# Eight row buffers for an expert gather, one half of an output projection taken block by block, and tile steps moved between two stages of a decoder layer

## The chip, the cores and the metric

The kernel runs on one core of one Trainium2 chip. The metric is the device time of one execution in microseconds (us), the median of several runs. The engines are PE (matmul), PEld (its weight load), DVE (vector), ACT (scalar), POOL (gpsimd) and SP (sync, which here only issues DMAs).

## The reference

One layer of a decoder, 512 tokens of width 1024, all in float32: a token mixing step (mLSTM heads beside sliding-window attention), a cross-attention into 256 memory tokens, and a PEER layer that retrieves experts. The change touches the end of the second and the third:

```python
h = h + memory_cross_attention(rmsnorm(h, g_cross[l]), rmsnorm(mem, g_mem[l]), ...)   # ends in o @ w_o
h = h + peer_ffn(rmsnorm(h, g_ffn[l]), w_pq[l], sub_keys1[l], sub_keys2[l], expert_down[l], expert_up[l])
return rmsnorm(h, g_final)

# inside peer_ffn, for each token: 8 heads, 16 experts of 128 x 128 per head
    eidx = jnp.take_along_axis(cand_i, pos, axis=-1)
    g = jax.nn.softmax(top_s, axis=-1)
    u = expert_down[eidx]
    a = jax.nn.gelu(jnp.einsum('thkd,td->thk', u, xb), approximate=False)
    coef = (g * a)
    return jnp.einsum('thk,thkd->td', coef, expert_up[eidx])
```

## The kernel before

The 512 tokens are four blocks of 128 (NB = 4). Products are made with three matmuls each (high part by high, high by low, low by high of operands split in two), so that float32 accuracy is kept. A split is a copy on ACT (the high part) and a subtraction on DVE (the low part).

`front` does the mixing, `cross` the cross-attention in the order of the string `CROSS`. Its last four items, x0 to x3, are `project`: two halves n of the output columns, two halves hf of the contraction; for each it loads a weight of 1 MB (`load_w`) and multiplies it with all four blocks; when hf is 1, `resid` adds the result to the residual `c.h`. Then `norm_T` normalizes each block (a square with a sum on ACT, `rsqrt` on DVE and POOL, a scaling on DVE), transposes it on PE and splits it into `xhi` and `xlo`.

The experts are done in two ways. Block 0 **gathers**: `gather` is a generator of 256 steps. Each step fetches one row per token (128 rows of 4 KB, 512 KB) with an indirect DMA issued by POOL (`fetch`, L685) into one of the buffers of tag `rows`, and one DVE operation consumes it: 128 dot products with `down` (L691), then 128 accumulations with `up` into `gacc` (L699, L701). Blocks 1 to 3 are **dense**: all 128 tiles of 128 experts are multiplied with all 384 tokens. A `Down` tile takes 8 k-steps of three matmuls (L757 to L759) and ends in a gelu; an `up_tile` multiplies the gelu by the gates and `up_mm` (L823 to L825) accumulates it. `down_t` and `up` come in loads of 1 MB for two tiles (`draw`, `uraw`).

The gates of the dense blocks are a matrix of 16384 experts by tokens. Block 1's is made by 128 scattering indirect DMAs on POOL (`scatter`, L614), those of blocks 2 and 3 by one-hot matmuls (`gating`, 32 steps for each block, L666; the one-hot operands come from ACT, L649 and L650, and DVE, L645 and L665).

The stages follow each other: `peer_topk` (queries, scores, top 16 of each head, on PE, ACT and above all DVE), `gating`, then the loop over `up_order()`. `Early.fill(k)` puts k k-steps of the first SP = 68 `Down` tiles between the steps of the first two: FRT[i] in each of the 16 `stage1` calls, FEND behind them, FGT with each gating step. Those tiles are spilled to DRAM and read again. The other 60 are made in the loop, five ahead (LEAD). In the loop, `step(ga, ...)` calls for gather steps, 256 spread over the first 122 of 128 tiles. Behind the loop stand the rest of the gather, the loads of the residual (`hb`) and four calls of `finish` (add, square, `rsqrt`, scaling, store), block 0 with `gacc` and then blocks 1 to 3, whose last two tiles' matmuls are held back and done block by block.

The order in the program is not the order on the engines: the framework plans each engine's queue beforehand (`schedule_with_timeline_sim=True`), by program order among what its plan takes to be ready, and inserts the waits. At run time each queue is in order. The rows buffers are memory slots: a fetch waits for the DVE operation that used the slot last. Tiles of a pool that opens where another closed wait for the last readers of that other one. On SP all loads and stores of the hardware queue stand in one line.

Of the kernel before, what the change touches and what calls it, by code (L numbers as in the profile page):

```python
# [21 lines left out]
P = 128  # L22
# [18 lines left out]
UG = 4  # L41
FRT = [16] + [24] * 15
FEND = 5 * KT
FGT = 2
SP = (sum(FRT) + FEND + (ND - NS) * 32 * FGT) // KT
SG = SP // UG
assert SP == SG * UG and (sum(FRT) + FEND) % KT == 0

GST = 122

# [6 lines left out]

CROSS = "m0 o0 K1 K0 V0 V1 n0 q0 s0 s1 q1 s2 p0 s3 p1 p2 p3 x0 x1 x2 x3"
HP = 400
# [345 lines left out]
def cross(c):  # L405
    nc, a, ps, xp = c.nc, c.a, c.ps, c.xp
    V, A, T = nc.vector, nc.scalar, nc.tensor
    qh, ql, probs, acc, wo = {}, {}, {}, {}, {}

# [50 lines left out]

    def project(i):
        n, hf = divmod(i, 2)
        if hf == 0:
            acc[n] = [ps.tile([P, 512], F32, tag="b", name=f"acc_t{b}") for b in range(NB)]
        w = load_w(c, a["w_xo"][n, hf], 512)
        for b in range(NB):
            mm3_tm(c, acc[n][b], w, slice(0, 512), hf, b)
            if hf:
                resid(c, b, n, acc[n][b])

    ops = {"n": norm, "K": lambda n: mem_k(c, n), "V": lambda n: mem_v(c, n), "m": lambda _: mem_norm(c),
           "o": lambda _: mix_out(c), "q": query, "s": scores, "p": values, "x": project}
    for op in CROSS.split():
        ops[op[0]](int(op[1]))


# [145 lines left out]

def gating(c, early):

    nc, ps, gs, mp = c.nc, c.ps, c.gs, c.mp
    V, A, T = nc.vector, nc.scalar, nc.tensor
    for b in range(NG + NS, NB):
# [24 lines left out]

        oh = [onehot(q) for q in range(3)]
        for q in range(32):
            if q % 8 == 0:
# [16 lines left out]
            with c.tc.issue_after(mm.ins):  # L672
                early.fill(FGT)


def gather(c):
# [6 lines left out]
    def fetch(src, j):  # L683
        r = gp.tile([P, D], F32, tag="rows", bufs=5, name="rows")
        G.indirect_dma_start(out=r, out_offset=None, in_=src,  # L685
                             in_offset=bass.IndirectOffsetOnAxis(ap=c.eidx[:, j:j + 1], axis=0))
        return r
# [328 lines left out]
def body(tc, a, out, dbg=None):  # L1016
# [3 lines left out]
    with ExitStack() as st:  # L1020
# [23 lines left out]
        with ExitStack() as hs:  # L1044
# [14 lines left out]
            c.xn0 = c.mp.tile([P, D], F32, name="xn0")  # L1059
            norm_T(c, [c.h[:, b] for b in range(NB)], D, c.xhi, c.xlo, xn0=c.xn0)  # L1060
            for b in range(NB):
                nc.sync.dma_start(c.hd[b], c.h[:, b])
        c.m2 = st.enter_context(pool("routes"))
        c.dp = st.enter_context(pool("down"))
        gel = []
# [10 lines left out]
        c.gl = st.enter_context(pool("gels"))  # L1076
        with pool("gather", side="right") as c.gp:
            with pool("gating") as c.gs:
                gating(c, early)
            ga = gather(c)  # L1080
            c.up = st.enter_context(pool("up"))
# [3 lines left out]
            acc = [[pst_[2 * b], pst_[2 * b + 1]] for b in range(ND)]  # L1085
            last = []
            for u, i2 in enumerate(up_order()):
                ahead(made_by(u) - len(gel))
                with tc.issue_after(c.dl.ins):
                    step(ga, 2 * P * (u + 1) // GST - 2 * P * u // GST)  # L1090
                parts = up_tile(c, u, i2, gel, acc)
                if u >= NK - 2:
                    last.append(parts)
                else:
                    for b in range(ND):
                        up_mm(c, u, parts, acc, b)
            step(ga, 2 * P)
            c.hb = []
            for b in range(NB):
                c.hb.append(c.gp.tile([P, D], F32, tag="rows", bufs=5, name="hb"))  # L1100
                nc.sync.dma_start(c.hb[b], c.hd[b])
# [29 lines left out]
def step(it, n):  # L1131
    for _ in range(n):
        next(it, None)
# [49 lines left out]
```

## Time and profile before

| | us |
|---|---|
| median of 3 runs (lowest to highest) | 1703.74 (1701.27 to 1706.47) |
| the profiled execution | 1698.9 |
| its span, first to last instruction | 1697.1 |
| PE busy in it | 1629.7 |
| DVE busy in it | 1236.8 |

The profiled execution lies 4.8 us below the median of the runs; what lies around its span is 1.8 us. "Busy" counts the time in which at least one instruction of an engine runs. PEclk is the TensorE clock that was granted, as a share of full speed. A wait is put down to what ended it. L numbers are lines of the kernel.

### The profile page before, as it was taken

What the parts mean: (1) busy time and instruction counts of PE and PEld (TensorE: products, weight loads), DVE (VectorE), ACT (ScalarE), POOL (GpSimd) and SP (SyncE); (2) the same over time, 40 slices, a digit from 0 to 9 for tenths busy, and PEclk for the clock granted to TensorE, in tenths of its full rate; (3) what the DMA queues carried; (4) which work ended last, traced back from release to release, by engine and by line L of the source; (5) the groups of instructions that cost most, each with busy time, mean ns of one, the idle gap of its engine ahead of it and who ended that gap; (6) DMA issues with size and microseconds to landing.
All of it is one profiled execution on the core that took longest, in us unless ns stands there. A gap on an engine that the chain in (4) does not pass through costs nothing.

```text
span 1697.1 us, 23023 instructions
## 1 busy us (share of the span) xinstructions
PE 1629.7 (96%) x8366; PEld 1424.7 (84%) x8368; DVE 1236.8 (73%) x2701; ACT 720.6 (42%) x1206; POOL 582.6 (34%) x427
## 2 busy tenths in 40 slices
PE   7999999999999999989999999999999999999990
PEld 5776588877999999989998888888888888888880
DVE  5536565464687876878858888877878788888897
ACT  5434544343445443478853333333333333333331
POOL 2000000000008686758003443334444344334563
PEclk9999999999999999999999999999999999999995
DMA  5136044224245554559769888989989999998887
GB/s 209 74 139 233 26 149 174 75 103 149 73 158 143 137 137 94 137 187 267 211 217 407 329 325 338 329 337 355 354 321 340 354 331 344 348 339 321 308 308 263
DMA packets 149105, 400.58 MB, mean 236 GB/s; under 512 B 28144, under 2 KB 62080, under 8 KB 136320
## 3 DMA queue, kind: packets, MB, share of 16 engines
q1 hardware_dynamic: 89232, 255.76, 41.6%
q0 software_dynamic: 55360, 134.32, 23.9%
q10 hardware_dynamic: 4400, 9.04, 1.5%
q8 instruction: 65, 1.06, 0.2%
q14 instruction: 48, 0.39, 0.1%
HBM read 356.28 MB, written 42.80 MB: 235 GB/s over the span
## 4 chain that ended last, share of the span: by engine, by line
PE 89%; issue 3%; POOL 2%; DVE 2%; DMA 2%; ACT 1%; DVEq 0%; POOLq 0%; ACTq 0%
PE acc_d L757 10%; PE acc_d L759 10%; PE acc_d L758 10%; PE acc_u L824 9%; PE acc_u L825 9%; PE acc_u L823 9%; PE acc_f L923 4%; PE acc_f L925 4%; PE acc_f L924 4%; PE w L666 3%; PE acc_t L936 2%; PE acc_t L938 2%; PE acc_t L937 2%; POOL rows L685 2%; DMA rows<-in_up_dram,eidx 1%
## 5 line engine op out<-in xcount | busy, mean ns | idle before, releaser
L757 PE MATMUL acc_d<-xhi,dh 128*128 128x384 f32 x1024 | 351.0, 343 | 2.8 <-ACT dh L708 1.8
L759 PE MATMUL acc_d<-xhi,dl 128*128 128x384 f32 x1024 | 345.1, 338 | 0.6 <-DVE dl L746 0.6
L758 PE MATMUL acc_d<-xlo,dh 128*128 128x384 f32 x1024 | 344.3, 336 | 0.0
L824 PE MATMUL acc_u<-ul,ch 128*128 128x512 f32 x762 | 297.8, 391 | 0.0
L825 PE MATMUL acc_u<-uh,cl 128*128 128x512 f32 x762 | 297.2, 391 | 0.0
L685 POOL DMA_INDIRECT rows<-in_down_r_dram,eidx x128 | 168.1, 1313 | 344.0 <-DVE dots L691 316.0
L614 POOL DMA_INDIRECT wd<-gg,ei x128 | 214.5, 1676 | 158.6 <-DVE ei L608 114.4
L823 PE MATMUL acc_u<-uh,ch 128*128 128x512 f32 x762 | 257.2, 390 | 0.0
L746 DVE TENSOR_TENSOR dl<-draw,dh 128x1024 fp32r<-128x1024 f32 x128 | 156.4, 1222 | 123.0 <-ACT dh L708 112.3
L685 POOL DMA_INDIRECT rows<-in_up_dram,eidx x128 | 175.7, 1373 | 199.6 <-DVE gacc L701 181.4
L708 ACT CAST dh<-draw 128x1024 fp32r<-128x1024 f32 x128 | 134.2, 1050 | 239.3 <-PE acc_d L758 201.3
L811 ACT CAST ch<-cf 128x384 fp32r<-128x384 f32 x127 | 65.2, 514 | 368.8 <-issue 334.2
L757 PEld LDWEIGHTS acc_d<-xhi,dh 128*128 128x128 f32 x1024 | 193.3, 189 | 7.1 <-ACT dh L708 2.2
L758 PEld LDWEIGHTS acc_d<-xlo,dh 128*128 128x128 f32 x1024 | 193.4, 189 | 3.7
L759 PEld LDWEIGHTS acc_d<-xhi,dl 128*128 128x128 f32 x1024 | 193.0, 189 | 2.6 <-DVE dl L746 1.2
L701 DVE SCALAR_TENSOR_TENSOR gacc<-rows,coef,gacc 128x1024 f32<-128x1024 f32 x127 | 162.6, 1280 | 7.5 <-DMA rows<-in_up_dram,eidx 6.5
L825 PEld LDWEIGHTS acc_u<-uh,cl 128*128 128x128 f32 x762 | 143.0, 188 | 29.4
L824 PEld LDWEIGHTS acc_u<-ul,ch 128*128 128x128 f32 x762 | 143.0, 188 | 28.9
L823 PEld LDWEIGHTS acc_u<-uh,ch 128*128 128x128 f32 x762 | 142.7, 188 | 27.1
L802 DVE TENSOR_TENSOR ul<-uraw,uh 128x1024 fp32r<-128x1024 f32 x127 | 154.9, 1220 | 7.8 <-ACT uh L708 6.7
L691 DVE CUSTOM_DVE_ANT_0 rows<-rows,xn 128x1024 f32<-128x1024 f32 x128 | 153.8, 1219 | 0.0
L812 DVE TENSOR_TENSOR cl<-cf,ch 128x384 fp32r<-128x384 f32 x127 | 70.7, 558 | 90.9 <-ACT ch L811 76.3
(333 smaller groups left out, 2659.9 us busy)
## 6 DMA issues: line engine op xcount, KB each, us to landing
draw<-in_down_t_dram SPq DMA_DIRECT2D x64, 1024.0 KB
uraw<-in_up_dram SPq DMA_DIRECT2D x64, 1024.0 KB
wt<-wd SPq DMA_DIRECT2D x96, 256.0 KB
wd<-stg SPq DMA_DIRECT2D x8, 2048.0 KB
gd<-gsp SPq DMA_DIRECT2D x17, 768.0 KB
gsr<-gd SPq DMA_DIRECT2D x17, 768.0 KB
wd<-zero ACTq DMA_DIRECT2D x1, 8192.0 KB
raw<-in_w_pq_dram SPq DMA_DIRECT2D x8, 1024.0 KB
```

Of the source, the lines that this page charges most:

```text
L614: i = G.indirect_dma_start(out=out, out_offset=bass.IndirectOffsetOnAxis(ap=ei[:, h, k:k + 1], axis=0), in_=c.gg[:, NG, hh, k:k + 1], in_o ...
L685: G.indirect_dma_start(out=r, out_offset=None, in_=src, in_offset=bass.IndirectOffsetOnAxis(ap=c.eidx[:, j:j + 1], axis=0))
L691: V.tensor_tensor_reduce(r, r, c.xn0, 1.0, 0.0, op0=ALU.mult, op1=ALU.add, accum_out=dots[:, j:j + 1])
L701: V.scalar_tensor_tensor(c.gacc, r, coef[:, j:j + 1], c.gacc, op0=ALU.mult, op1=ALU.add)
L746: c.dl = nc.vector.tensor_tensor(self.lo, raw, f32(self.hi), op=ALU.subtract)
L757: T.matmul(acc[:, :TD], self.hi[:, ks], c.xhi[:, k, NG * P:], start=(k == 0), stop=False)
L758: T.matmul(acc[:, :TD], self.hi[:, ks], c.xlo[:, k, NG * P:], start=False, stop=False)
L759: T.matmul(acc[:, :TD], self.lo[:, ks], c.xhi[:, k, NG * P:], start=False, stop=(k == KT - 1))
L802: V.tensor_tensor(lo, raw, f32(hi), op=ALU.subtract)
L823: T.matmul(acc[b][n], ch[:, t], hi[:, d], start=st, stop=False)
L824: T.matmul(acc[b][n], ch[:, t], lo[:, d], start=False, stop=False)
L825: T.matmul(acc[b][n], cl[:, t], hi[:, d], start=False, stop=sp)
```

## The change

- `rows` gets 8 buffers in place of 5, and the generator is made before `gating`, which gets it as an argument: in its last block (b = 3) every fourth step calls one gather step, 8 in all. The loop then spreads 248 steps over its first 122 tiles.
- x0 to x3 leave `CROSS`, and `project` becomes a function that runs after the pools of `cross` have closed. Its first half (n = 0) is as before. The weights of the second half get buffers of their own (`w2`), and each block does both halves of the contraction, `resid` and then, as the argument of `norm_T`, its normalization, before the next block begins. The pools `routes` and `down` open ahead of it.
- FRT falls from 24 to 20 k-steps in 14 of 16 places and FEND from 40 to 24; FGT rises from 2 to 3, and FGT0 = 8 k-steps are put between the first three one-hot tiles and the first gating step. SP stays 68: 544 k-steps either way.

```diff
-FRT = [16] + [24] * 15
-FEND = 5 * KT
-FGT = 2
-SP = (sum(FRT) + FEND + (ND - NS) * 32 * FGT) // KT
+FRT = [16] + [20] * 14 + [24]
+FEND = 3 * KT
+FGT0 = KT
+FGT = 3
+SP = (sum(FRT) + FEND + FGT0 + (ND - NS) * 32 * FGT) // KT
+GEV = 4
-CROSS = "m0 o0 K1 K0 V0 V1 n0 q0 s0 s1 q1 s2 p0 s3 p1 p2 p3 x0 x1 x2 x3"
+CROSS = "m0 o0 K1 K0 V0 V1 n0 q0 s0 s1 q1 s2 p0 s3 p1 p2 p3"
-    def project(i):
-        n, hf = divmod(i, 2)
-        if hf == 0:
-            acc[n] = [ps.tile([P, 512], F32, tag="b", name=f"acc_t{b}") for b in range(NB)]
-        w = load_w(c, a["w_xo"][n, hf], 512)
-        for b in range(NB):
-            mm3_tm(c, acc[n][b], w, slice(0, 512), hf, b)
-            if hf:
-                resid(c, b, n, acc[n][b])
+def project(c):
+    ps, a = c.ps, c.a
+    acc = [ps.tile([P, 512], F32, tag="b", name=f"acc_t{b}") for b in range(NB)]
+    w2 = []
+    for hf in range(2):
+        w = load_w(c, a["w_xo"][0, hf], 512)
+        for b in range(NB):
+            mm3_tm(c, acc[b], w, slice(0, 512), hf, b)
+            if hf:
+                resid(c, b, 0, acc[b])
+        w2.append(load_w(c, a["w_xo"][1, hf], 512, pool=c.w2))
+    def block(b):
+        acc = ps.tile([P, 512], F32, tag="b", name=f"acc_t{b}")
+        for hf in range(2):
+            mm3_tm(c, acc, w2[hf], slice(0, 512), hf, b)
+        resid(c, b, 1, acc)
+        return c.h[:, b]
+    norm_T(c, [lambda b=b: block(b) for b in range(NB)], D, c.xhi, c.xlo, xn0=c.xn0)
...
 def gating(c, early, ga):
+        if b == NG + NS:
+            early.fill(FGT0)
         for q in range(32):
...
             with c.tc.issue_after(mm.ins):
                 early.fill(FGT)
+                if b == NB - 1 and q % GEV == GEV - 1:
+                    step(ga, 1)
...
-        r = gp.tile([P, D], F32, tag="rows", bufs=5, name="rows")
+        r = gp.tile([P, D], F32, tag="rows", bufs=8, name="rows")
...
-            norm_T(c, [c.h[:, b] for b in range(NB)], D, c.xhi, c.xlo, xn0=c.xn0)
+            c.m2 = st.enter_context(pool("routes"))
+            c.dp = st.enter_context(pool("down"))
+            with pool("project") as c.w2:
+                project(c)
...
+            ga = gather(c)
             with pool("gating") as c.gs:
-                gating(c, early)
-            ga = gather(c)
+                gating(c, early, ga)
...
+            g0 = 32 // GEV
-                    step(ga, 2 * P * (u + 1) // GST - 2 * P * u // GST)
+                    step(ga, (2 * P - g0) * (u + 1) // GST - (2 * P - g0) * u // GST)
...
-                c.hb.append(c.gp.tile([P, D], F32, tag="rows", bufs=5, name="hb"))
+                c.hb.append(c.gp.tile([P, D], F32, tag="rows", bufs=8, name="hb"))
```

## Rows read from the trace of the kernel before

**Rows 1.** The page: busy time by engine, and the shares of the chain that ended last.
```profile
PE 1629.7 (96%) x8366; PEld 1424.7 (84%) x8368; DVE 1236.8 (73%) x2701; ACT 720.6 (42%) x1206; POOL 582.6 (34%) x427
...
PE 89%; issue 3%; POOL 2%; DVE 2%; DMA 2%; ACT 1%; DVEq 0%; POOLq 0%; ACTq 0%
```

**Rows 2.** Busy time by stretch, cut at the seams of the stages: mixing and cross-attention to the end of the projection's matmuls, the seam to the top-k, the top-k, the seam to the gating, the gating, the seam to the loop, the loop, what lies behind PE's last matmul. The columns are the stretch, its length, the busy time of PE, PEld, DVE, ACT and POOL, each with its instructions, the granted clock, the DMA share and GB/s.
```profile
0.00:407.00 407.00, 393.26 (x1880) 300.82 (x1883) 216.22 (x453) 178.08 (x349) 20.78 (x38) 1.00 0.37 132
407.00:420.00 13.00, 8.93 (x50) 8.09 (x49) 8.71 (x10) 5.90 (x9) 0.90 (x2) 0.74 0.55 213
420.00:739.00 319.00, 319.00 (x1794) 303.68 (x1793) 240.03 (x1082) 146.25 (x192) 161.11 (x97) 1.00 0.46 127
739.00:750.00 11.00, 5.83 (x27) 5.16 (x25) 5.74 (x13) 7.88 (x22) 9.17 (x7) 0.69 1.01 402
750.00:877.00 127.00, 126.95 (x905) 126.23 (x903) 103.80 (x293) 105.49 (x245) 50.16 (x31) 1.00 0.71 203
877.00:905.00 28.00, 24.52 (x128) 23.50 (x128) 15.84 (x22) 10.71 (x16) 8.25 (x5) 0.94 0.99 344
905.00:1656.00 751.00, 751.00 (x3593) 657.19 (x3591) 617.75 (x793) 261.12 (x360) 316.91 (x236) 1.00 0.90 337
1656.00:1697.10 41.10, 0.17 (x1) 0.00 (x0) 28.76 (x38) 5.18 (x16) 15.34 (x15) 0.56 0.72 263
```

**Rows 3.** The timeline at the end: start, duration, engine, line, operation; in brackets the idle time before it and what ended it.
```profile
1655.79 0.39 PE L825 MATMUL acc_u<-xlo 128*128 128x512 f32 x1
...
1679.26 1.28 DVE L701 SCALAR_TENSOR_TENSOR gacc<-rows,coef,gacc 128x1024 f32<-128x1024 f32 x1 [1.32 <-DMA rows<-in_up_dram,eidx]
1680.58 1.29 DVE L836 TENSOR_TENSOR hb<-hb,gacc 128x512 f32<-128x512 f32 x2
...
1684.38 1.28 DVE L836 TENSOR_TENSOR hb<-hb,acc_u 128x512 f32<-128x512 f32 x2
...
1685.63 2.73 DVE L842 SCALAR_TENSOR_TENSOR hb<-hb,frst,xn 128x512 f32<-128x512 f32 x4
...
1689.42 2.74 DVE L842 SCALAR_TENSOR_TENSOR hb<-hb,frst,xn 128x512 f32<-128x512 f32 x4 [0.60 <-POOL frst L854]
```

**Rows 4.** The accumulations of the gather alone (L701, one instruction for each row), by stretch: stretch, length, DVE busy with the count, granted clock, DMA share, GB/s.
```profile
1600.00:1650.00 50.00, 25.13 (x20) 1.00 0.89 320
...
905.00:1656.00 751.00, 144.79 (x114) 1.00 0.90 337
1656.00:1697.10 41.10, 17.81 (x14) 0.56 0.72 263
```

**Rows 5.** The dot products of the gather alone (L691, two instructions for each row), in a stretch of the loop.
```profile
950.00:1250.00 300.00, 110.12 (x182) 1.00 0.90 337
```

**Rows 6.** The gating product of each up tile (L809, one for each tile) in the same stretch.
```profile
950.00:1250.00 300.00, 28.29 (x51) 1.00 0.90 337
```

**Rows 7.** Who waited for whom in the loop, 905 to 1655: us in total, times, longest.
```profile
POOL rows L685 <- DVE dots L691: 238.7, 90, 9.3
POOL rows L685 <- DVE gacc L701: 179.9, 92, 7.6
...
ACT uh L708 <- DMA uraw<-in_up_dram: 0.9, 1, 0.9
```

**Rows 8.** Busy time in the loop's busiest stretch for the DMA engines (columns as in Rows 2).
```profile
900.00:950.00 50.00, 50.00 (x246) 44.34 (x245) 38.52 (x57) 18.53 (x26) 15.59 (x15) 1.00 0.99 383
```

**Rows 9.** What PE waited for, over the whole span.
```profile
PE tp_n L894 <- DVE rsq L853: 4.0, 1, 4.0
PE w L666 <- ACT oh L650: 3.7, 1, 3.7
```

**Rows 10.** Busy time in slices of 5 us at the two seams ahead of the top-k and of the gating (columns as in Rows 2).
```profile
410.00:415.00 5.00, 2.68 (x11) 2.17 (x12) 4.86 (x7) 2.50 (x5) 0.55 (x1) 0.66 0.69 248
415.00:420.00 5.00, 5.00 (x30) 5.00 (x31) 1.30 (x2) 0.82 (x2) 0.00 (x0) 0.66 0.14 57
...
740.00:745.00 5.00, 0.82 (x3) 0.41 (x3) 3.46 (x7) 4.96 (x19) 4.20 (x3) 0.77 1.03 399
745.00:750.00 5.00, 4.61 (x20) 4.61 (x21) 2.28 (x6) 1.96 (x4) 4.08 (x4) 0.55 1.00 402
```

**Rows 11.** The timeline from the last scores of the top-k to the first gating matmul.
```profile
714.60 0.59 ACT L511 COPY ss<-s 128x512 f32<-128x512 f32 x1
...
735.69 0.35 DVE L570 TENSOR_TENSOR I<-eq 128x64 f32<-128x64 bf16 x2
...
739.02 0.38 PE L631 MATMUL tp_i<-ident,I 128*128 128x128 f32 x2
...
745.39 2.07 PE L666 MATMUL w<-oh,oh 128*128 128x128 f32 x8 [3.70 <-ACT oh L650]
```

**Rows 12.** The timeline of PE: the first matmul of two k-steps that follow each other.
```profile
734.85 0.33 PE L757 MATMUL acc_d<-xhi,dh 128*128 128x384 f32 x1
...
735.37 0.33 PE L757 MATMUL acc_d<-xhi,dh 128*128 128x384 f32 x1
```

**Rows 13.** The chain that ended last, in order of time: two gating steps that follow each other (start, us, what).
```profile
751.45 0.89 PE w L666 x8
753.39 0.89 PE w L666 x8
```

**Rows 14.** A wait of POOL in the top-k, 425 to 740: its queue had done all but the last scattering group, and its next instruction, a first row fetch, had to wait.
```profile
POOL rows L685 <- DVE ei L608: 16.2, 1, 16.2
```

More of the change, by code (lines that the diff above doesn't have):

```diff
@@ L407, in cross @@
     V, A, T = nc.vector, nc.scalar, nc.tensor
-    qh, ql, probs, acc, wo = {}, {}, {}, {}, {}
+    qh, ql, probs = {}, {}, {}
     def norm(_):
@@ L459, in values @@
             split_psum(c, c.xhi[:, k], c.xlo[:, k], o)
-    def project(i):
-        n, hf = divmod(i, 2)
-        if hf == 0:
-            acc[n] = [ps.tile([P, 512], F32, tag="b", name=f"acc_t{b}") for b in range(NB)]
-        w = load_w(c, a["w_xo"][n, hf], 512)
-        for b in range(NB):
-            mm3_tm(c, acc[n][b], w, slice(0, 512), hf, b)
-            if hf:
-                resid(c, b, n, acc[n][b])
     ops = {"n": norm, "K": lambda n: mem_k(c, n), "V": lambda n: mem_v(c, n), "m": lambda _: mem_norm(c),
-           "o": lambda _: mix_out(c), "q": query, "s": scores, "p": values, "x": project}
+           "o": lambda _: mix_out(c), "q": query, "s": scores, "p": values}
     for op in CROSS.split():
         ops[op[0]](int(op[1]))
+def project(c):
[16 more added lines that the diff above has]
+    norm_T(c, [lambda b=b: block(b) for b in range(NB)], D, c.xhi, c.xlo, xn0=c.xn0)
 def peer_topk(c, early):
@@ L620, in scatter, with gating @@
             c.sc.setdefault(hh, []).append(i)
-def gating(c, early):
+def gating(c, early, ga):
     nc, ps, gs, mp = c.nc, c.ps, c.gs, c.mp
@@ L1059, in body @@
             c.xn0 = c.mp.tile([P, D], F32, name="xn0")
-            norm_T(c, [c.h[:, b] for b in range(NB)], D, c.xhi, c.xlo, xn0=c.xn0)
+            c.m2 = st.enter_context(pool("routes"))
+            c.dp = st.enter_context(pool("down"))
+            with pool("project") as c.w2:
+                project(c)
             for b in range(NB):
                 nc.sync.dma_start(c.hd[b], c.h[:, b])
-        c.m2 = st.enter_context(pool("routes"))
-        c.dp = st.enter_context(pool("down"))
         gel = []
```

## The prediction

> **What bounds the kernel now.** I read the page first, then busy time by stage, then the end of the timeline, and only then the waits. On the page PE is busy 1629.7 of 1697.1 us and carries 89% of the chain [rows 1]. The 67.4 us in which it is not are unevenly spread [rows 2]: 13.7 in mixing and cross-attention, 4.1 at the seam to the top-k, 0 in the top-k, 5.2 at the seam to the gating, 0 in the gating, 3.5 at the seam to the loop, 0 in the 751 us of the loop, and 40.9 behind PE's last matmul. The matmuls are the same before and after: 544 spilled k-steps, the same projection, the same loop. So the change can gain only where PE idles or runs at the lower clock, above all in those 40.9 us, and lose only by opening new gaps.
>
> What fills the tail: PE ends at 1656.18, the last accumulation of the gather at 1680.54, the span at 1697.1 [rows 3]. 14 of the 128 accumulations run behind PE's last matmul, 1.75 us for each [rows 4]; `finish` of four blocks takes the last 16.6 us. The tail is block 0's gather, late by some 14 rows, and then four finishes in a line that three of them need not have waited in.
>
> Why it is late: the program calls 256 steps in 122 tiles, 2.10 a tile. On the DVE queue there are 91 rows to 51 tiles, 1.78 a tile [rows 5, 6]. That order was fixed by the planner, and POOL shows what the gather is short of: in the loop POOL waits 238.7 and 179.9 us for the DVE operation that frees a buffer [rows 7], while DVE hardly waits for a row. Five slots turn over in 5 x 300/91 = 16.5 us. When no new `Down` tiles are loaded any more the pace rises to 20 rows in 50 us [rows 4], so in the plan a slot's round trip grows with what else is being loaded.
>
> **Eight buffers, eight steps earlier, 248 in the loop (the large term).** The loop now asks for 248/122 = 2.03 rows a tile, 2.89 us a row at 5.88 us a tile [rows 6], in place of the 3.30 that it got. With eight slots this allows a round trip of 23 us where five had 16.5. I take it that the asked pace is met, or nearly: 10% more rows from 60% more slots. Then the gather ends beside PE's last tiles, block 0's finish too, and blocks 1 and 2 finish while block 3's last matmuls run. What stays behind PE's last matmul is one block: from the first addition of `finish` to the first scaling 5.05 us (1680.58 to 1685.63), of which the first addition, 0.64, lies ahead; two scalings, 1.4; and from the last scaling's end, 1692.16, to the end of the span 4.9 [rows 3]. That is 10.7, say 11, in place of 41: **-30**.
>
> DVE has room: it is 82% busy in the loop [rows 2], the extra 0.25 rows a tile cost 0.3 us of 5.9 (1.22 to 1.28 us each), and in the stretch with 20 accumulations PE lost nothing [rows 2, 4]. The eight early steps cost DVE 10 us in a gating of 127 us of which 104 are busy, and that stage becomes longer. Their rows are the first eight fetched; POOL begins to fetch at the top-k's end and the block that consumes them begins some 80 us later, so I cost a wait for them at nothing. If one came late, the one-hot operations (L665) queued behind it on DVE would be late, and PE's gating matmuls with them.
>
> DMA: the loop moves 337 GB/s on average at a DMA share of 0.90 [rows 2]. The rows left to fetch in the loop hardly change: before 242 consumed less 5 fetched ahead plus those in flight, about 240; after 256 less 16. The pace while draws run rises by 0.524 MB x (1/2.89 - 1/3.30) = 22 GB/s. The bound from the rows is 383 GB/s at a share of 0.99, reached at the start of the loop with PE at 50.0 of 50 us [rows 8]. 337 + 22 = 359 fits under it, with little to spare.
>
> The Trainium skill (DMA: Bandwidth & Descriptors, Bandwidth, "Where 436 GB/s comes from") says that transfers from HBM are bound at about 358 GB/s per core, since two cores share a stack. By that ceiling the pace would only just be reached and any slip would stay, which is rival A. The rows reach 383 and 402 GB/s [rows 2, 8], so this trace, with one core running, doesn't show that ceiling.
>
> **The second half of the projection block by block.** Now all four blocks end together, and their norms follow: PE waits 4.0 us [rows 9] and then at a granted clock of 0.66 from 410 to 420 [rows 10], that is for part of it at 1.2 in place of 2.4 GHz. In 407 to 420 PE idles 4.07 us; I put the clock at another 2.5 us (5 us of work in the second slice at 0.66 is 1.7 lost, the busy 2.7 of the first 0.9). Block by block, the norm of b runs on ACT, DVE and POOL beside the 24 matmuls of b+1 (5.5 us of PE). Behind block 3 its own norm remains: addition, square, `rsqrt`, scaling, some 4 us, then transposes. Its cover is the first query products, which need blocks 0 and 1 only. The weights of the top-k find their buffers free earlier, since the second half has its own. Those w2 tiles lie where `cross` had its operands, so their splits, and ACT's and DVE's queues behind them, wait for `cross`'s last reader; the first half of the projection, some 20 us of matmuls, covers that. Gain 4.07 + 2.5 less a remainder of 0.5: **-6**; bounds -7 and, if the cover fails, 0.
>
> **Tile steps moved.** A k-step is 0.52 us of PE [rows 12]. 72 of them leave the top-k (14 x 4 + 16), 37.6 us, and as many reach the gating (8 + 64): no net PE time. The top-k shrinks from 319 to some 281 us; DVE does nine fewer `dl` there, 229 busy of 281, 81% after 75%. A gating step grows from 1.94 [rows 13] to 2.46 us, which leaves ACT, 105 of 127 us busy [rows 2], more room than now. POOL's scattering has its own slack: it waited 16.2 us ahead of the last group [rows 14], and the last two heads lose at most 6.3 us of PE work. On SP, each `draw` may now queue behind a store of gates that waits for its eighth step; loads run two tiles ahead, some 13 us, which hides the 2 to 6 us.
>
> The seam to the gating has two halves. Ahead of the transposes PE fills 24.4 us (714.6 to 739.0) while DVE needs 21.4 for the last head's indices (714.6 to 736.0) [rows 11]. FEND's 16 fewer steps take 8.3 us of that cover, FGT0's 8 give 4.2 back if the planner lets them run ahead of the transposes, and DVE loses two `dl`, 2.4 us: 20.3 against 19.0, even. Behind the transposes the wait for the first one-hot tile (3.7 of 5.2 us idle [rows 9]) and the clock of 0.55 to 0.77 [rows 10], some 2 us, are what FGT0 would hide, if it is still there. I expect that it is mostly used up: **-1**; bounds +5 (1 or 2 us in each of the few gaps) and -7. The 3.5 us at the seam to the loop (a `draw` behind the last store of gates) stay: 0; bounds -5 (the clock with them) and +3.
>
> **Sum.** -30 - 6 - 1 + 1 (small new waits) = -36: a span of 1661, an execution of 1663 against 1698.9, and on the scale of the median 1703.74 - 36 = **1668 us**.
>
> **Rivals.**
> A. *The gather still ends last*, because its pace is set by the loads and not by the slots. For: the pace rose when the draws stopped [rows 4], the share of 0.90 to 0.99. Against: POOL always waited for a slot. Then the rows left at PE's end are 14 less 8 done early and up to 3 held in more buffers, 3 to 6, at 1.75 us, and the whole 16.6 us of finishes: a tail of 22 to 27, -14 to -19. With -6: 1679 to 1684.
> B. *Less cover costs PE gaps in the top-k and the gating.* For: DVE is in order and its bursts of top-16 stay as long while the fill shrinks from 12.5 to 10.4 us a head half. Against: PE's zero idle in 319 us. One us in each of 16 calls is 16 us: 1684.
> C. *Slower: the gather's eight outstanding fetches put the loop's loads late.* Each `uraw` or `draw` then ends in a PE gap. Priced: 64 `uraw` loads, 1 us each, +64: 1732. It turns the sign from 0.56 us a load on. For: the DMA share. Against: 383 GB/s without one PE wait [rows 8]; ACT waited 0.9 us once for a `uraw` [rows 7].
> D. *It doesn't do what it says*: the planner's DVE order keeps the finishes behind the old lag and the projection's blocks wait for the w2 splits; only the eight early rows count, 14 us: 1690.
>
> **How the numbers follow.** Chances: forecast 0.60 (1654 to 1676), A 0.17, B 0.10, C 0.06, D 0.07. The range reaches from 1654 (-30 - 7 - 7 - 5 = -49, nearly all bounds at their good end) to 1686, which takes in A and B. A measurement tells about 0.3%, 5 us, from no change. Faster by more than that: the forecast, A, B and most of D, 0.89; within it 0.04; slower 0.07.
>
> **What would show it.** Right: the last L701 ends before or within some 5 us of PE's last matmul and the tail falls from 41 to about 11; PE no longer waits for `rsq` at the seam to the top-k and the clock stays full there; PE stays at 100% in top-k, gating and loop; rows to tiles near 2.03 on DVE. Wrong: L701 operations behind PE's end (A), PE waits on `dl`, `qf` or one-hot tiles (B), PE waits on `uh` or `dh` released by a DMA (C).

## The result, and the profile after

The changed kernel takes **1724.30 us** (1722.64 to 1727.19) against 1705.11 for the kernel before on the same chip: a ratio of 1.0116, 95% interval 1.009 to 1.0142. It is slower by 19 us; 1668 had been forecast. The profiled execution took 1724.66 us, with a span of 1723.0.

I first cut both spans at the same five points, read in the tile view as first and last starts of PE's matmuls: the last `ox` (end of cross-attention's values), the first `tp_i` (end of the top-k), the first and the last `acc_u` (the loop), the end. All runs of this document stand here, in us; the last columns are the median and its ratio to the kernel before.

| run | to last `ox` | to `tp_i` | to first `acc_u` | loop | tail | span | median | ratio (interval) |
|---|---|---|---|---|---|---|---|---|
| before | 366.7 | 372.3 | 168.7 | 748.1 | 41.3 | 1697.1 | 1705.1 | 1 |
| after | 374.2 | 332.8 | 227.7 | 776.5 | 11.8 | 1723.0 | 1724.3 | 1.0116 (1.009 to 1.0142) |
| e1_anchor_dve | 366.9 | 332.8 | 191.7 | 782.5 | 11.8 | 1685.7 | 1691.5 | 0.9915 (0.989 to 0.9939) |
| e2_buffers_alone | 374.3 | 371.3 | 169.4 | 776.7 | 11.8 | 1703.5 | 1704.5 | 0.999 (0.9977 to 1.0003) |
| e3_project_alone | 371.1 | 364.8 | 167.8 | 748.1 | 42.3 | 1694.1 | 1698.4 | 0.9953 (0.9936 to 0.997) |
| e4_fill_alone | 369.7 | 339.1 | 190.0 | 756.0 | 39.1 | 1693.9 | 1697.9 | 0.995 (0.9934 to 0.9967) |
| e5_old_fill | 374.3 | 364.8 | 192.7 | 773.8 | 11.8 | 1717.4 | 1719.9 | 1.0082 (1.0065 to 1.0099) |
| e6_both_anchors | 366.4 | 332.7 | 189.9 | 773.1 | 12.0 | 1674.1 | 1678.3 | 0.9842 (0.9821 to 0.9863) |
| e7_buffers_pace | 370.7 | 371.5 | 168.9 | 771.0 | 12.1 | 1694.2 | 1697.9 | 0.9972 (0.9955 to 0.999) |
| e8_no_early_pace | 372.5 | 332.8 | 188.4 | 776.9 | 11.8 | 1682.4 | 1685.4 | 0.9879 (0.9862 to 0.9895) |
| e9_gst100 | 373.0 | 332.8 | 188.6 | 776.1 | 11.8 | 1682.3 | 1683.0 | 0.9857 (0.984 to 0.9875) |
| e11_drop32 | 373.0 | 332.8 | 188.8 | 760.8 | 9.3 | 1664.7 | 1665.8 | 0.976 (0.9743 to 0.9776) |
| e12_spread | 373.0 | 332.8 | 188.4 | 776.1 | 11.8 | 1682.1 | 1684.3 | 0.9871 (0.9854 to 0.9887) |
| e13_one_column | 366.6 | 332.8 | 189.7 | 768.9 | 11.8 | 1669.8 | 1673.4 | 0.9818 (0.9794 to 0.9841) |
| e14_no_fetch | 373.4 | 332.8 | 188.8 | 763.0 | 9.4 | 1667.4 | 1668.0 | 0.9771 (0.9742 to 0.98) |
| e15_uraw3 | 366.8 | 332.7 | 189.9 | 755.3 | 28.1 | 1672.8 | 1676.8 | 0.9837 (0.9811 to 0.9863) |
| e16_rows6 | 374.6 | 332.8 | 188.9 | 759.2 | 19.4 | 1674.9 | 1675.7 | 0.9818 (0.9791 to 0.9844) |
| e17_rows7_uraw3 | 370.9 | 332.8 | 188.7 | 755.3 | 25.4 | 1673.1 | 1674.6 | 0.9826 (0.9802 to 0.985) |

After against before: tail -29.5, as forecast; top-k stretch -39.5; gating stretch +59.0; loop +28.4; the front +7.5. Moving 72 k-steps past `tp_i` explains -33.2, +21.3 and, in the loop, +7.9, since the run with these steps alone has them too (e4). Those 7.9 are no slower loop: behind the first `acc_u` of e4 stand 45 matmuls more (3622 in place of 3577). The projection explains another -7.5 ahead of `tp_i` (e3). What is left over are two losses: some 36 us in the gating and 20.5 in the loop.

PE's waits of after over the whole span (us in total, times, longest) name both:

```profile
PE w L684 <- DVE oh L683: 31.4, 6, 17.1
...
PE acc_u L843 <- ACT uh L728: 8.7, 6, 1.9
PE acc_u L844 <- DVE ul L822: 5.9, 3, 2.0
```

The `rsq` wait of [rows 9] is gone, and a wait for one-hot tiles is there. Busy time by stretch of after (columns as in [rows 2]: the hole, the rest of the gating, the loop, its closing tiles, the matmuls behind the gather, the tail):

```profile
706.00:780.00 74.00, 37.42 (x198) 34.92 (x197) 32.22 (x80) 26.84 (x64) 61.81 (x41) 0.75 0.59 159
780.00:912.00 132.00, 132.00 (x914) 132.00 (x913) 94.22 (x252) 99.24 (x217) 26.49 (x17) 1.00 0.74 231
...
945.00:1580.00 635.00, 627.80 (x3051) 554.34 (x3050) 530.66 (x677) 220.01 (x301) 293.95 (x217) 1.00 0.92 351
1580.00:1640.00 60.00, 49.95 (x215) 39.42 (x214) 55.77 (x62) 18.91 (x27) 22.70 (x17) 1.00 0.94 367
1640.00:1711.60 71.60, 71.54 (x316) 58.92 (x314) 42.44 (x61) 27.34 (x44) 1.12 (x2) 1.00 0.38 133
1711.60:1723.00 11.40, 0.00 (x0) 0.00 (x0) 4.11 (x10) 1.33 (x4) 1.10 (x2) 0.71 0.36 137
```

PE loses 36.6 of the 74 us at the start of the gating, nothing in the rest of it, 7.2 in the loop to 1580, 10 in the next 60 us. In those 60 DVE is busy 93% and the DMA share is 0.94; right behind, with the gather over, both fall (59%, 0.38) and PE is full. The gather now ends some 74 us ahead of PE:

```profile
L721 DVE SCALAR_TENSOR_TENSOR gacc<-rows,coef,gacc x127: 1271/1279/1305, 1283.8 to 1636.7; 128x1024 f32<-128x1024 f32 x127
```

The hole itself, in DVE's timeline of after:

```profile
726.74 1.23 DVE L711 CUSTOM_DVE_ANT_0 rows<-rows,xn 128x1024 f32<-128x1024 f32 x1 [15.20 <-DMA rows<-in_down_r_dram,eidx]
...
727.89 0.34 DVE L683 TENSOR_SCALAR oh<-iota,I2T,gT 128x128 f32<-128x128 f32 x1
...
762.13 1.23 DVE L711 CUSTOM_DVE_ANT_0 rows<-rows,xn 128x1024 f32<-128x1024 f32 x1 [18.98 <-DMA rows<-in_down_r_dram,eidx]
```

and POOL's beside it:

```profile
720.42 1.56 POOL L630 DMA_INDIRECT wd<-gg,ei  x1 [0.31 <-issue]
722.28 1.04 POOL L705 DMA_INDIRECT rows<-in_down_r_dram,eidx  x1 [0.30 <-issue]
...
726.13 1.61 POOL L630 DMA_INDIRECT wd<-gg,ei  x1 [0.30 <-issue]
...
755.96 1.54 POOL L630 DMA_INDIRECT wd<-gg,ei  x1 [0.30 <-issue]
757.81 1.00 POOL L705 DMA_INDIRECT rows<-in_down_r_dram,eidx  x1 [0.30 <-issue]
```

The early dot products stand among the one-hot tiles (L683) of the first gating block, not of the last one, where the program calls them. DVE waits 15.2 and 19.0 us for rows with the one-hot tiles queued behind it: POOL comes late to the first three fetches, since it is still scattering, and 16 more scatters (some 1.55 us each and 0.3 between) stand ahead of the fourth.

The loop's loss can be read by following each of PE's waits back: to the operation that ended it, to what stood ahead of that one on its engine's queue, and so on. In the closing tiles of after (ACT, then PE, then DVE):

```profile
1613.79 0.51 ACT L831 CAST ch<-cf 128x384 fp32r<-128x384 f32 x1 [3.57 <-PE acc_u L844]
1614.20 1.99 ACT L728 CAST uh<-uraw 128x1024 fp32r<-128x1024 f32 x2
...
1615.30 1.66 PE L843 MATMUL acc_u<-uh,ch 128*128 128x512 f32 x6 [1.37 <-ACT uh L728]
1618.94 0.50 PE L844 MATMUL acc_u<-ul,ch 128*128 128x512 f32 x1 [1.98 <-DVE ul L822]
...
1614.80 1.28 DVE L721 SCALAR_TENSOR_TENSOR gacc<-rows,coef,gacc 128x1024 f32<-128x1024 f32 x1
1616.00 0.55 DVE L829 TENSOR_TENSOR cf<-gsr,wt 128x384 f32<-128x384 f32 x1
1616.47 1.28 DVE L721 SCALAR_TENSOR_TENSOR gacc<-rows,coef,gacc 128x1024 f32<-128x1024 f32 x1
1617.67 1.22 DVE L822 TENSOR_TENSOR ul<-uraw,uh 128x1024 fp32r<-128x1024 f32 x1
```

PE waits 1.37 us for `uh`, the high part of an `up` tile. The cast that makes it did not wait for its load: on ACT's queue it stood behind the cast of `ch`, the high part of the gated gelu, and that one waited 3.57 us for PE's own matmuls to give back one of two `ch` buffers. The 1.98 us are for a subtraction that stood on DVE behind two accumulations of rows. In the kernel before, the two casts alternate in these tiles, and `ch` does not wait for PE:

```profile
1619.60 0.51 ACT L811 CAST ch<-cf 128x384 fp32r<-128x384 f32 x1 [2.91 <-issue]
1620.02 1.05 ACT L708 CAST uh<-uraw 128x1024 fp32r<-128x1024 f32 x1
```

Of the 18.3 us that PE idles in the loop of after, no wait ends at a load. Those for `uh` lead back to a `ch`, one to a `dh` (the same cast of a `Down` tile), that waits for PE; those for `ul` to row accumulations on DVE; the rest, for `gel` and `ch`, to the same queues. ACT itself waits 3.2 us for `uraw` there, and none of that releases a wait of PE.

### The profile page after: what moved, and what is told of

Read it like the earlier page. It is cut to its first block, busy times and chain, and to the rows that moved or that the text cites. A ratio compares the mean times of both kernels' runs of the same rounds, so it can differ in the third digit from the quotient of the medians.

```text
span 1723.0 us, 22949 instructions
## 1 busy us (share of the span) xinstructions
PE 1640.4 (95%) x8366; PEld 1428.0 (83%) x8368; DVE 1236.0 (72%) x2701; ACT 724.5 (42%) x1206; POOL 602.9 (35%) x427
## 5 line engine op out<-in xcount | busy, mean ns | idle before, releaser
L705 POOL DMA_INDIRECT rows<-in_down_r_dram,eidx x128 | 177.7, 1388 | 296.5 <-DVE dots L711 276.4
L630 POOL DMA_INDIRECT wd<-gg,ei x128 | 230.4, 1800 | 138.1 <-DVE ei L624 87.3
L705 POOL DMA_INDIRECT rows<-in_up_dram,eidx x128 | 170.5, 1332 | 189.7 <-DVE gacc L721 167.9
L843 PE MATMUL acc_u<-uh,ch 128*128 128x512 f32 x762 | 216.0, 392 | 9.9 <-ACT uh L728 8.7
L843 PEld LDWEIGHTS acc_u<-uh,ch 128*128 128x128 f32 x762 | 141.9, 188 | 39.5 <-ACT uh L728 11.2
```

What stands on the lines that cost most here:

```text
L630: i = G.indirect_dma_start(out=out, out_offset=bass.IndirectOffsetOnAxis(ap=ei[:, h, k:k + 1], axis=0), in_=c.gg[:, NG, hh, k:k + 1], in_o ...
L705: G.indirect_dma_start(out=r, out_offset=None, in_=src, in_offset=bass.IndirectOffsetOnAxis(ap=c.eidx[:, j:j + 1], axis=0))
L843: T.matmul(acc[b][n], ch[:, t], hi[:, d], start=st, stop=False)
```

## The experiments

The theory after the first look: (1) the hole is an order fault on DVE, since the early steps are placed behind a PE instruction, which holds nothing on DVE's queue; (2) the loop's loss is either order (the gather too early among the tiles) or eight fetches under way beside the loop's loads (rival C). The first four runs separate the parts.

**e1: the early steps behind DVE's own one-hot operation** (the edits shown from here on are cut to the lines that matter).
```diff
-                V.tensor_scalar(o2, c.iota, i2[:, t:t + 1], ...)
+                od = V.tensor_scalar(o2, c.iota, i2[:, t:t + 1], ...)
-                if b == NB - 1 and q % GEV == GEV - 1:
-                    step(ga, 1)
+            if b == NB - 1 and q % GEV == GEV - 1:
+                with c.tc.issue_after(od.ins):
+                    step(ga, 1)
```


> The changed kernel with one difference: the eight gather steps of the gating are queued behind the last one-hot operation on DVE of their own gating step, where the change queued them behind that step's matmul on PE, which holds nothing on DVE. Theory (the three DVE waits for rows, 15.2 + 0.8 + 19.0 us ahead of the first gating steps, are the loss): the hole of 36.6 us PE idle between 706 and 780 shrinks to the 5 us of before and the low clock with it (some 7 us): 1724 - 38 = 1686, 0.978 of the changed kernel and 0.989 of the one before; the DVE wait for rows in the gating is 0. Rival (POOL's scattering, late by 16 us since the top-k is shorter, holds the gating in some other way as well): above 1710.

Measured: 1691.5 where 1686 was expected, the gating stretch 36.0 us shorter than after's and the loop 6.0 longer, so that 30 are left by the spans behind the front. The first dot product is read out at 795 in place of 728, and PE works through the same 74 us of gating (columns as in [rows 2]):

```profile
699.00:773.00 74.00, 68.83 (x454) 68.15 (x453) 50.65 (x134) 56.14 (x129) 62.42 (x39) 0.95 0.83 244
```

**e2: eight row buffers alone, in the kernel before.**
```diff
-        r = gp.tile([P, D], F32, tag="rows", bufs=5, name="rows")
+        r = gp.tile([P, D], F32, tag="rows", bufs=8, name="rows")
```


> The kernel before with eight row buffers in place of five and nothing else. Theory (the tail's gain of 29 us comes from the buffers, the 17 us that PE lost in the loop come with them, because DVE gets the rows earlier than it can hide them): tail 41 to some 11 us, loop idle 0 to 5 to 17 us, 1705 - 13 to - 25 = 1680 to 1692. Rival 1 (the tail was shortened by the eight early steps instead): tail stays above 25 us, 1690 to 1700. Rival 2 (the loop's loss comes from the late start after the gating's hole, not from the buffers): loop idle 0, 1675.

Measured: 1704.5, no gain, where 1680 to 1692 was expected. The tail falls by 29.5 and the loop grows by 28.6. The loop in e2, with the matmuls that took 748.10 us without a gap before:

```profile
915.00:1691.70 776.70, 755.11 (x3575) 655.27 (x3574) 636.33 (x816) 267.00 (x371) 327.22 (x244) 0.99 0.88 334
```

21.6 us are idle, and PE is busy 7.0 us longer, of which some 5 are the lower clock in two stretches behind such waits:

```profile
1240.00:1265.00 25.00, 20.60 (x77) 16.09 (x76) 18.53 (x29) 6.36 (x9) 10.74 (x9) 0.86 0.87 324
1590.00:1615.00 25.00, 20.02 (x79) 15.42 (x77) 23.90 (x26) 6.82 (x10) 14.25 (x10) 0.93 1.00 382
```

So the loop's loss comes with the buffers alone. Followed back, PE's waits lead to the queues as in after: some 10 us of `uh` behind `ch`, 7 of `ul` behind row operations on DVE, 4 of `gel`, none to a load. What the buffers changed is how often `ch` waits for PE, in the kernel before and in e2 (us in total, times, longest):

```profile
ACT ch L811 <- PE acc_u L824: 32.0, 10, 4.7
...
ACT ch L811 <- PE acc_u L824: 272.4, 88, 6.7
```

**e3: the projection alone; e4: the moved tile steps alone** (each the kernel before with that part of the change).

> The kernel before with the projection taken block by block (and its pools opened ahead) and nothing else. Theory (the seam to the top-k costs 4.07 us idle and some 2.5 us of low clock): 1705 - 6 = 1699, PE waits no longer for rsqrt there. Rival (the waits for the memory of the cross-attention's operands come in its place): 1705 or above.

> The kernel before with the new FRT, FEND, FGT0 and FGT and nothing else: no gather step in the gating, five buffers. Theory (the shorter top-k makes POOL late by some 16 us, but late fetches cost only if DVE waits for them): no hole, 1705 + -4; PE idle at the seam to the gating about 5 us. Rival (the shorter cover itself opens the hole, by POOL's backlog or by DVE's last head): 15 to 35 us idle at that seam, 1720 or above.

Measured: e3 1698.4 (-7.3), its top-k stretch 7.5 us shorter. e4 1697.9 (-7.9; by the stretches behind the front -6.2): no hole opens without early gather steps. Of the 6.2, 2.2 lie in the tail and some 3 at the seam to the loop, where PE idles 2.3 us in place of 3.5 and the granted clock stays at 1.00 (before, 0.79 and 0.87 from 890 to 900). The wait of 3.7 us for the first one-hot tile is still there.

**e5: after, with the tile steps of before.**
```diff
-FRT = [16] + [20] * 14 + [24]
-FEND = 3 * KT
-FGT0 = KT
-FGT = 3
+FRT = [16] + [24] * 15
+FEND = 5 * KT
+FGT0 = 0
+FGT = 2
```


> The change with the distribution of the Down tiles of before (24 k-steps a block in top-k, five tiles' steps at the seam, two steps with a gating step): POOL then has the scatters of before in the order of before. Theory (the hole in gating is that VectorE's dots of the early steps stand ahead of the one-hot tiles, and POOL's fetches stand behind its scatters): the 16 scatters of a head still stand between the third and the fourth fetch, so a dot still waits about 19 us for its rows, while the first wait (15.2 us) shrinks as POOL is less late; PE loses 15 to 37 us in gating, and the loop keeps its 25 us of waits: 1715 to 1740 us. Rival (the k-steps moved into gating make the hole): without them the hole is gone, PE's wait on w from the one-hot tiles falls under 5 us, and the time is 1685 to 1700.

Measured: 1719.9. The gating stretch is 24.9 us longer than in e3, which has the same steps. The hole so needs only the early dot products; the moved steps add 11 us to it. DVE waits 35.0 us for its rows there in after and 19.8 in e5, whose gating begins 32 us later. PE's waits of e5:

```profile
PE w L684 <- DVE oh L683: 17.7, 4, 13.4
```

**e6: both orders by DVE's own operations.** e1, and in the loop the steps behind the previous up tile's last subtraction, in place of a Down tile's, which is made five or more tiles ahead.
```diff
-    V.tensor_tensor(cl, cf, f32(ch), op=ALU.subtract)
+    c.cli = V.tensor_tensor(cl, cf, f32(ch), op=ALU.subtract)
-                with tc.issue_after(c.dl.ins):
+                with tc.issue_after(c.cli.ins if u else c.dl.ins):
```


> The change with the early steps behind VectorE's own last one-hot operation of their gating step, and in the loop each tile's steps behind the previous up tile's last subtraction on VectorE, in place of the last subtraction of a Down tile five or more tiles ahead. Theory (the loop lost its 20 to 28 us because VectorE's order has the dots too early among the tiles): PE's idle time in the loop falls from about 20 us to under 6, and the time is 1691 less 14 to 24: 1667 to 1677. Rival 1 (eight fetches under way put the loop's loads late): the order doesn't matter, the loop stays at 775 to 785 us and the time at 1688 to 1695. Rival 2 (the rows now come so late in the loop that the sum is again what ends last): loop shorter, tail of 25 to 40 us, 1685 to 1700.

**e7: e2 with the loop's half of that edit; e8: e6 without the early steps.**

> The kernel before with eight row buffers, and the loop's steps behind the previous up tile's last subtraction on VectorE. Theory (order of VectorE): the loop is 748 to 757 us as before and the tail 12 to 20, so 1676 to 1688. Rival 1 (eight fetches under way): as with the eight buffers alone, a loop of about 777 and 1701 to 1707. Rival 2 (rows too late): a loop of 750, a tail of 30 to 40 us, 1695 to 1706.

> The change without the eight early steps in the gating (the fetches are still begun there), and the loop's steps behind the previous up tile's last subtraction. Theory: no hole in gating, since no dot stands among the one-hot tiles; the loop without the 20 to 28 us; 1668 to 1680. Against the run with both anchors it tells what eight early steps are worth: 8 of 256 rows at some 2.9 us each are 23 us of the gather's chain, but only if that chain ends last; if the tail is about 12 us in both, nothing (within 4 us). Rival (the early steps are what frees the tail): a tail of 25 us or more here, 1685 to 1695.

Measured: e6 1678.3, just outside what its theory allowed, with 12.9 us idle in the loop where under 6 was expected. The loop gets 9.4 of its 26.5 us back (773.1; e4's division of work needs 756.0). e7 1697.9, between theory and rival: 771.0, 5.7 back of 28.6. So this edit of the order gives back the smaller part of the loop's loss. e8, 1685.4, misses its 1668 to 1680 and lies 7 us above e6; 6.1 of the 8.3 us between the spans lie in the front, where both kernels are alike, so that the early steps are worth about 2 us.

**e9, e12: where the rest is lost.** In e6 PE's last Down matmul starts at 1541.6, 120 us before the loop ends (before: at 1610.6, 45 us), and 11.3 us of its idle time lie between 1540 and 1640. I thought that DVE was short there. e9 makes the gather's steps earlier, e12 holds the Down tiles back.
```diff
-GST = 122
+GST = 100
```
```diff
-                ahead(made_by(u) - len(gel))
+                with tc.issue_after(c.upi.ins if u else c.dl.ins):
+                    ahead(made_by(u) - len(gel))
```


> The run with both anchors, with the loop's steps spread over 100 up tiles in place of 122; in VectorE's order the last of the 128 weighted row additions then stands behind up tile 111 in place of 122, and 28 of them behind tile 99 in place of 45. Theory (VectorE is short in the closing tiles: the last Down tile stands before up tile 102 of PE's order, from there a tile is 18 matmuls of some 0.215 us, 3.9 us, while VectorE has 2.08 us of the tile's own work and two additions of 1.2 us, 4.5 us; 18 us are lost so in the last 140 us of the loop): fewer additions there, a loop of 762 to 768 in place of 773, and 1665 to 1674. Rival (eight fetches under way, or the loads): the closing tiles lose as before, 1676 to 1682.

> The run with both anchors, with each Down tile of the loop held on PE behind the previous up tile's last matmul, so that the last Down tile stands before up tile 117 of PE's order in place of 102 (all rows are gathered as in the run with both anchors). Theory (VectorE is short where up tiles come without a Down tile): only some ten tiles are left without one, so of the 18 us about 8 to 14 come back: a loop of 759 to 766, 1664 to 1671. Rival (a Down tile at its place in the program comes late with its operands, and PE waits for dl or gel): PE's waits of acc_d rise over 10 us and the time is 1678 to 1695.

Measured: 1683.0 and 1684.3, both misses for the theory, with loops of 776.1. (e12's rival had the time; the waits it named, for `acc_d`, stay under 1 us.) The last Down matmul of e12 is at 1625, as meant, and PE is full in its closing tiles; the idle time had only moved, to stretches all along the loop. That spoke against a shortage of DVE in one place. One of these waits of e12, 2.28 us for `uh` at 971.31, leads back on ACT to a `dh` that waits for PE's own Down matmuls, which the edit holds back:

```profile
968.89 1.04 ACT L729 CAST dh<-draw 128x1024 fp32r<-128x1024 f32 x1 [3.68 <-PE acc_d L779]
```

**e11, e13, e14: the last 32 of 256 steps, without both halves, without the addition, without the fetch** (in e6). These three tell where time goes and are no candidates: e11 leaves 32 of the 128 rows out of block 0's sum, e13 leaves out 1023 of the 1024 columns of those rows, e14 adds one row 32 times in their place. The edits of e13 and e14:
```diff
+            w = 1 if j >= 96 else D                        # e13
-            V.scalar_tensor_tensor(c.gacc, r, coef[:, j:j + 1], c.gacc, op0=ALU.mult, op1=ALU.add)
+            V.scalar_tensor_tensor(c.gacc[:, :w], r[:, :w], coef[:, j:j + 1], c.gacc[:, :w], op0=ALU.mult, op1=ALU.add)
-        r = fetch(c.a["up"], j)                            # e14
+        if j < 96:
+            r = fetch(c.a["up"], j)
```


> The run with both anchors without the last 32 of the 256 gather steps: their 32 fetches and 32 weighted additions on VectorE are left out (the first block's sum then lacks 32 of its 128 rows). Theory (VectorE is short in the closing tiles): 32 x 1.2 us are gone from just there, PE waits no more, the loop is 754 to 759 us, and the time 1658 to 1664. Rival (the tiles' own operands, their loads or the eight buffers set the pace there): the loop stays at 768 to 774 and the time at 1672 to 1679.

> The run with both anchors, with the last 32 weighted additions cut from 1024 columns to one (1023 of 1024 columns of those 32 rows are left out of the first block's sum); all 256 fetches, their buffers and the order of the steps stay. Theory (VectorE's 32 x 1.2 us in the closing tiles are what PE waits for): as with the 32 steps dropped, a loop of 757 to 764 us and 1662 to 1669. Rival (the last 32 fetches themselves, 16 MB of the DMA engines and 32 issues on POOL beside the tiles' loads): the loop stays at 768 to 774 us and the time at 1674 to 1681.

> The run with both anchors, with the last 32 fetches left out: the last 32 weighted additions all read the row fetched last (those 32 rows of the first block's sum are wrong so), and keep their 1.2 us each on VectorE. Theory 1 (the DMA engines are full in the closing tiles): a loop of 760 to 766 us in place of 773, and 1665 to 1671. Theory 2 (VectorE alone): a loop of 769 to 774, 1674 to 1680. If both limit, each alone gives a part (4 us for VectorE, measured) and this run lies between the two.

The loop is 17.1 us over its 756.0 in e6, 12.9 without the additions, 7.0 without the fetches, 4.8 without either. Leaving out the fetches is worth 10 us, DVE's additions 4, both 12: the fetches are the greater part, and e13's theory (a loop of 757 to 764) fell. e14 met its first theory; e11 lies just outside its own, 754 to 759. The closing tiles of e13 and, below, of e14 (columns as in [rows 2]; then the time from issue to landing of the tiles' 1 MB loads, in the tile view of `uraw` over 1540 to 1645):

```profile
1540.00:1640.00 100.00, 92.50 (x401) 74.04 (x400) 61.42 (x111) 34.52 (x50) 33.34 (x31) 1.00 0.93 360
...
DMA to landing us min/median/max: 4.8/10.1/13.6
```

```profile
1540.00:1640.00 100.00, 96.62 (x427) 79.64 (x426) 93.84 (x106) 34.80 (x48) 0.73 (x1) 1.00 0.56 205
...
DMA to landing us min/median/max: 4.8/4.9/7.5
```

DVE is busy 61% in e13 and PE idles 7.5 us; it is busy 94% in e14 and PE idles 3.4. So the share of DVE does not decide. The loads land later in e13, but of the six waits for `uh` that make up the 7.5 us only one, of 0.67 us, ends at a load. In the other five, of 1.37 us each, the load had landed 1.6 to 6.2 us before its cast began, and the cast stood behind a `ch`:

```profile
1595.82 0.51 ACT L833 CAST ch<-cf 128x384 fp32r<-128x384 f32 x1 [3.57 <-PE acc_u L846]
1596.24 1.99 ACT L730 CAST uh<-uraw 128x1024 fp32r<-128x1024 f32 x2
```

In e14 `ch` and `uh` alternate in most of these tiles, as in the kernel before. Leaving out the fetches so changed the order on ACT together with the traffic, and the 10 us can't be divided between the two.

The Trainium skill (DMA: Bandwidth & Descriptors, "Anatomy of one DMA") fits the time of a DMA that POOL issues as 2.0 us and its bytes at 436 GB/s, which by that page would be an estimate of 4.4 us for 1 MB. The loads here are issued by SP; e14's median of 4.9 us, at a DMA share of 0.56, lies near it, and e13's 10.1 was taken beside row fetches.

**e15, e16, e17: fewer fetches under way, or a load buffer more** (in e6: six row buffers and three for `uraw`; six and two; seven and three with `RING = 8`).
```diff
-        r = gp.tile([P, D], F32, tag="rows", bufs=8, name="rows")
+        r = gp.tile([P, D], F32, tag="rows", bufs=6, name="rows")       # e15, e16; 7 in e17
-        c.uraw = up.tile([P, GRP, D], F32, tag="uraw", bufs=2, name="uraw")
+        c.uraw = up.tile([P, GRP, D], F32, tag="uraw", bufs=3, name="uraw")   # e15, e17
```


> The run with both anchors with six row buffers in place of eight, and three buffers in place of two for the up tiles' pairs of 1 MB. Theory (late loads at the DMA engines' limit): PE's waits of acc_u for uh (6.8 us) fall under 3, the loop is 762 to 768 us, and unless the gather is late again for two buffers less the time is 1668 to 1676. Rival (VectorE, or the gather's chain with six buffers): a loop over 768 or a tail over 20 us, 1679 to 1695.

> The run with both anchors with six row buffers in place of eight, load buffers as they were. Theory 1 (fewer fetches under way leave the loads in time): a loop of 754 to 760 us, a tail of 26 to 32, and 1675 to 1680, as with the third load buffer. Theory 2 (the third load buffer did it): PE waits for uh again, a loop of 762 to 773, 1682 to 1695.

> The run with both anchors with seven row buffers, three load buffers and eight in place of ten buffers of finished Down tiles. If a seventh row buffer gives the gather back part of its pace and the third load buffer keeps PE from waiting: a loop of 755 to 761 and a tail of 16 to 24, 1668 to 1674. If loop and tail only trade the same transfers: the sum of loop and tail stays at 783 to 786, and the time at 1674 to 1680.

Measured: loops of 755.3, 759.2 and 755.3 and tails of 28.1, 19.4 and 25.4. Six row buffers with no other edit take the loop's loss from 17.1 us to 3.2 and give 7.4 back in the tail. e16 met its first theory, with a shorter tail than the 26 to 32 expected; e15 has a better loop than expected and misses its 1668 to 1676 by 0.8; the loop and tail of e17 add up to 780.7, under the 783 to 786 of the theory whose time it met.

Two things go with the buffers here. Loads land sooner (over 940 to 1030 a median of 7.5 us in e16 against 9.7 in e12, which has the Down tiles at nearly the same place), and ACT's order is another one. `ch` waits for PE 60 times in e6, 32 in e12, 16 in e16, 6 in e15 and 5 in e17; both `uh` casts of a load stand back to back for 17 of the loop's loads in e6, 14 in e12, 6 in e16 and none in e15 and e17. PE's waits of e6 and e12, followed back, end at the order and none at a load.

The fastest full kernels, e15 to e17, lie within their spread of each other at 1674.6 to 1676.8, 0.982 to 0.984 of the kernel before and 48 us under the change as it was made. Each trades loop against tail; none has both short.

## Why the prediction was wrong, by its steps

- **The tail, -30: right, though not by the pace worked out.** -29.5; one block's finish stays, 11.4 us behind PE's last matmul where 11 was worked out. But the gather does not end beside PE's last tiles. From 950 to 1250 DVE has 99 rows to 46 tiles, 2.15 a tile where 2.03 was asked, and it ends some 74 us ahead of PE. The amount holds because one finish is left over whenever the gather ends ahead. (From 3.30 to 2.89 us a row is 14% more rows, where the prediction says 10%.)
- **Block by block, -6: right.** -7.3 alone; the wait for `rsq` went as described, a little past the bound of -7.
- **Tile steps, -1: within the bounds, and gained elsewhere.** -6.2 by stages. That FGT0 would be mostly used up held: the wait for the first one-hot tile is still 3.7 us. Some 3 us came at the seam to the loop, which stood at 0, and 2.2 in the tail.
- **Early steps, "I cost a wait for them at nothing": the first step that failed.** It rested on the program's place for them, the last gating block, 80 us behind the fetches. On DVE's queue they stood in the first block. The consequence was named (one-hot tiles and PE's gating behind it), its cause was not looked for: what an order edge to a PE instruction holds on another engine. "POOL's scattering has its own slack: it waited 16.2 us" failed with it: with the top-k shorter POOL is late by about as much (in after it reaches its first fetch with no wait but the 0.30 us between issues), and a head's 16 scatters stand ahead of the fourth fetch. Price: 36.0 us of gating (e1), 24.9 with the old steps (e5). PE's waits for one-hot tiles were to tell rival B, less cover; e4, where only the cover moves, opens no hole.
- **The loop, nothing for DVE and DMA: the second step that failed.** 20.5 us in after, 28.6 with the buffers alone (e2). "DVE has room" and "359 fits under it" compared shares and means over the loop. What PE waits for is the order on the queues: casts on ACT that stand behind a `ch` or `dh` waiting for PE itself, and subtractions on DVE behind row operations. With eight row buffers the plan had another order there (88 waits of `ch` for PE in e2, 10 before). Rival C had the sign, at a chance of 0.06, but its mechanism, PE gaps that end at a DMA, is not what happened: none of after's does. Such waits came to 2.1 us in e7 and 0.7 in e13, small beside their losses. My second theory, DVE short in the closing tiles, fell too: leaving out its additions gave 4 of 12 us there.
- The terms add up: -7.5 (projection) - 6.2 (tile steps, 2.2 of it in the tail) - 27.3 (the rest of the tail) + 36.0 + 20.5 + 7.5 (the front, below) = 23.0, of 25.9 between the spans.

Open is why the plan with eight row buffers puts the casts in that order; it may count on later loads, but no run shows what the plan counted on. Open is also how much of what e14 and e16 gained is traffic and how much order, since both change with the fetches. The run that would tell, eight row buffers with ACT's order of the kernel before, was not made.

## What to carry to other kernels

An early step is only as early as its queue says: before costing a moved step at nothing, look for what holds it on its own engine, and for what stands ahead of its producer on that engine's queue. More buffers on one engine's path can change the planned order on engines that never touch them: here three more row buffers changed ACT's. Shares and means do not show that; a wait followed back through the queues, until it ends at a DMA, at an issue or at the waiting engine itself, does. A gain in the tail is to be looked for again in the loop, by running that part alone.

## What the runs showed of the hardware

The front, whose instructions are alike in all these kernels, took 366.4 to 374.6 us to the last `ox`. In the profile of before the granted clock stays at 1.00 from 130 to 160 us; in that of after it falls to 0.50, 1.2 GHz, over 140 to 160, with PE busy 10.00 of the 10 us ahead of it in both (before, then after; columns as in [rows 2]):

```profile
130.00:140.00 10.00, 10.00 (x45) 6.45 (x44) 3.93 (x9) 3.14 (x4) 0.00 (x0) 1.00 0.26 99
140.00:150.00 10.00, 8.56 (x52) 5.96 (x52) 9.43 (x57) 6.76 (x33) 1.02 (x1) 1.00 1.02 348
150.00:160.00 10.00, 8.59 (x43) 5.43 (x43) 7.56 (x28) 4.99 (x22) 1.01 (x1) 1.00 1.05 406
```

```profile
130.00:140.00 10.00, 10.00 (x43) 6.46 (x43) 3.77 (x9) 3.15 (x4) 0.00 (x0) 0.98 0.25 93
140.00:150.00 10.00, 9.97 (x41) 7.05 (x39) 8.27 (x47) 5.61 (x28) 1.02 (x1) 0.50 1.02 349
150.00:160.00 10.00, 9.22 (x26) 5.35 (x25) 6.48 (x30) 6.00 (x26) 1.01 (x1) 0.50 1.05 407
```

The fronts of before and after differ by 7.5 us. In the five profiles where the clock stays at 1.00 there (before, e1, e6, e13, e15) the front takes 366.4 to 366.9 us, in the other thirteen, where it falls, 369.7 to 374.6. No edit touches the front; stages behind it are compared by their own lengths for that reason.
